# Two more up tiles computed in seven products, with a new order of the MLP and new places for the adding transfers

## The chip, the cores and the metric

The kernel runs on one core of a Trainium2 chip. The metric is the device time of one execution in microseconds. It was taken three times for the kernel before the change: 725.09, 725.68 and 725.84 us, with the median 725.68 us. One further execution was recorded by the hardware profiler; all rows below come from it.

## The reference

One layer of an encoder over 512 tokens of width 1024, all in float32: a norm, one input projection into three groups of attention heads, their attention, an output projection into the residual; then the MLP that the change touches, and a gated embedding of the input.

```python
def conv_gated_mlp(h, w_up, conv_w, conv_b, w_down):
    u = h @ w_up                                   # 512x1024 by 1024x5632
    up = jnp.pad(u, ((0, 0), (CONV_WIDTH - 1, 0), (0, 0)))
    c = conv_b
    for j in range(CONV_WIDTH):                    # causal, width 3, per channel
        c = c + conv_w[j] * up[:, j:j + S]
    gate, val = jnp.split(c, 2, axis=-1)
    return (jax.nn.silu(gate) * val) @ w_down      # 512x2816 by 2816x1024
...
    h = h + jnp.concatenate([o_a, o_b, o_c], axis=-1) @ w_out[i]
    h = h + conv_gated_mlp(rms_norm(h, ln_ffn[i]), w_up[i], conv_w[i], conv_b[i], w_down[i])
```

## The kernel before

**Products.** Each float32 operand is split into two parts of a narrower type: a rounded one (`hi`, made by ACT) and the remainder (`lo`, made by DVE). A product is three matmuls on PE: hi by hi, hi by lo, lo by hi. The weights come from DRAM into one of six raw tiles of 128x768 (`w_raw`), are split into `w_hi` and `w_lo`, and the raw tile is then free for the next load. Loads are issued by SP in one fixed order, each as soon as its raw tile is free.

**Up tiles.** The 2816 hidden channels are 22 tiles of 128. An up tile needs the 128 columns of the gate half and the 128 of the value half, for all 512 tokens. A plain tile (`up_plain`, accumulators named `u`) takes 2 halves x 8 blocks of rows x 3 = 48 matmuls that are 512 wide, and three raw tiles of weights (768, 768 and 512 columns). A tile in seven products (`up_seven`, accumulators `sX`, `sY`, `sZ`) sees the same work as a product of 2x2 block matrices (even and odd blocks of rows, gate and value, first and second half of the tokens) and takes seven block products in the place of eight: 7 x 4 x 3 = 84 matmuls that are 256 wide. It needs five raw tiles: two with the plain blocks, and three with sums of blocks (768, 768, 512 columns). The sums of the activations (`xh`, `xl`) are made once, whatever the number of such tiles. The results are put together by four copies on ACT and four additions on DVE into `su`, from which the convolution reads. Tiles 6 and 10 are computed so.

**Sums in DRAM.** The sums of weight blocks are not there at the start. Four transfers, DRAM to DRAM, issued by SP during the attention, copy blocks into a DRAM tensor (`usum` for an up tile, 4 x 256 KB; `dsum` for a phase of the down product, 4 x 768 KB or 4 x 512 KB). Later three transfers on POOL's queue add other blocks onto them in DRAM; the second and third read what the first has written. Before each, POOL runs a tiny `tok` instruction that reads the result of a finished up tile, so that the adding transfer does not start earlier. `COPY_SLOTS` (line 71) spreads all copies evenly over the units 20 to 45 of the attention; a copy stands in SP's order behind the last load issued by then (line 837). `ADD_AT` (line 72) gives for each add the number of finished up tiles behind which it stands.

**Down products.** Up tiles are taken together in four phases (tiles 0 to 5, 6 to 11, 12 to 17, 18 to 21), and each phase and half of the output columns is again seven products (`dn_X`, `dn_Y`, `dn_Z`), which are added to the residual `h` on DVE. Phase 0 makes its sums of weights on POOL (`w_raw<-w_raw,w_raw`), phases 1 to 3 read `dsum`.

**The order.** PE's order in the MLP is written out by hand in `ORDER` (line 49): a letter takes the next piece of a plain tile (P, three per tile), of a tile in seven products (S, six per tile) or of the down products (D, one product). Which tiles are plain follows from the same string (`tiles_of`, line 52). The orders of ACT, DVE, POOL and SP in the MLP follow from a planner at the end of the kernel: it gives each task a due time from PE's order and takes, again and again, the most urgent of those that could start. In the attention another scheduler sets the order. Nearly all instructions are recorded by a helper and carry its line, L108; the tiles' names tell them apart.

Of the kernel before, what the change touches and what calls it, by code (L numbers as in the profile page):

```python
# [45 lines left out]
PHASES = (0, 6, 12, 18, 22)  # L46


ORDER = ("PPPPPPPPPPPSSSPSSPSPPPDPDDDDDDPPPSSSSSDSDDDDDDPPPPPPPPPDPDDDDDDDPDPPDPPDDDDPPPPPPPPPPPPPPPPPPP")


def tiles_of(order):

    f, n, tiles = 2, {"P": 0, "S": 0}, {"P": [], "S": []}
    for c in order:
        if c in n:
            if n[c] == 0:
                tiles[c].append(f)
                f += 1
            n[c] = (n[c] + 1) % {"P": 3, "S": 6}[c]  # L60
    assert f == NF and not any(n.values()), (f, n)
    return tiles["P"], tiles["S"]


PLAIN, SEVEN = tiles_of(ORDER)

# [2 lines left out]
_sums = sorted([(f, "u", f) for f in SEVEN] + [(PHASES[ph + 1] + 3, "d", ph) for ph in range(NEAR, len(PHASES) - 1)])  # L69

COPY_SLOTS = (20, 46)
ADD_AT = (0, 0, 1, 1, 2, 2, 5, 5, 8, 9, 10, 12, 12, 12, 13)
COPIES, LATE = {}, {}
for _i, _q in enumerate(_sums):
    for _k in range(4):
        COPIES.setdefault(COPY_SLOTS[0] + (4 * _i + _k) * (COPY_SLOTS[1] - COPY_SLOTS[0]) // (4 * len(_sums)), []).append((_q[1:], _k))
    for _k in range(3):
        LATE.setdefault(ADD_AT[3 * _i + _k], []).append((_q[1:], _k))


@with_exitstack
def kernel(ctx: ExitStack, tc: tile.TileContext, x, xt0, xt, pt_in, small, g_ffn_in, bias_c,
# [1223 lines left out]
    def up_plain(f):  # L1306

        ws, w, more = plain_weights(f)
        us = Slot("z"), Slot("s")

        def some(g, ks):
            def do():
                c = g * NF + f
                if ks[0] == 0:
                    U[c] = bank("zs"[g], f"u{c}")
                for k in ks:
                    mm3(U[c], *w(g, k), Th[k // 4][:, k % 4, :], Tl[k // 4][:, k % 4, :], k == 0, k == KD - 1)
            return do

        for g in range(2):  # L1320
            pe_task(36, some(g, range(6)), [more()], (), [us[g]])
            yield
        last = []
        more()
        for g in range(2):
            last.append([pe_task(12, some(g, range(6, KD)), [ws[2]], (), (), [us[g]])])
        ff_chain(f, None, last, ((us[0],), (us[1],)))
        yield
# [213 lines left out]
    def down_pieces():  # L1542
        for ph in range(2):
            for n in range(2):
                d = Down((ph,), n, DT)
                for what in PRODUCTS:
                    d.product(what)
                    yield

        for n, whats in enumerate(FIRST):  # L1550
            DL.append(Down((2, 3), n, ({"X": "z", "Y": "s", "Z": "o"} if n else DT)))
            for what in whats:
                DL[n].product(what, (2,), False)
                yield

    DL = []
    pieces = {"P": (f for f in PLAIN for _ in up_plain(f)), "S": (f for f in SEVEN for _ in up_seven(f)), "D": down_pieces()}
    for c in ORDER:
        next(pieces[c])
# [231 lines left out]
```

## Time and profile before

| | before |
|---|---|
| median of three runs | 725.68 us |
| profiled execution | 725.56 us, of which the span is 723.8 us |
| PE busy | 706.4 us, 98% of the span |
| DVE, ACT, POOL busy | 536.2, 391.8, 220.2 us |
| mean granted clock | 0.996 |
| DMA queue of SP (q1) | 38,028 packets, 89.51 MB, 38.6% of 16 engines' span |
| DMA queue of POOL (q0) | 5,008 packets, 16.78 MB, 12.8% |
| attention until the first `u` matmul | 313.67 us |

The busy time of PE is modelled from pipelined matmuls, so its gaps are best read from the starts of neighbouring matmuls: 0.233 us apart when 512 wide, 0.119 us when 256 wide. A row of the chain or the timeline gives the start, the length, the engine and line, the operation and tiles; "[0.96 <-DMA ...]" is idle time ahead and what ended it. A row of a table of stretches gives the busy time of PE, PEld, DVE, ACT and POOL with the number of instructions, then the granted clock, the share of the DMA engines and GB/s.

### The profile page before, as it was taken

The numbers are of one execution on the slowest core, as the hardware profiler recorded it, in microseconds if no ns is written. First come the engines' busy times: TensorE is split into PE (matmuls) and PEld (weight loads), VectorE is DVE, ScalarE is ACT, GpSimd is POOL, SyncE is SP. The second block draws the span as 40 slices with busy tenths as digits, with TensorE's granted clock in tenths as the row PEclk, the third lists the DMA queues.
The fourth block names the chain that finished last, engine by engine and source line by source line (L and its number), as shares of the span: only waits on it lengthen the run. The fifth ranks groups of instructions, "written<-read, shape, count | busy, mean of one in ns | idle before, by whom it ended". The sixth has DMA issues, their size and how long they took to land.

```text
span 723.8 us, 11826 instructions
## 1 busy us (share of the span) xinstructions
PE 706.4 (98%) x4182; PEld 631.9 (87%) x4182; DVE 536.2 (74%) x1085; ACT 391.8 (54%) x739; POOL 220.2 (30%) x339
## 2 busy tenths in 40 slices
PE   9898999999999999999999999999999999999997
PEld 8897989988999887889889899988988888999886
DVE  8578787887878854857776998897857677677542
ACT  6646775865766663556354363645434445435721
POOL 4675675766665640200200505100010000000400
PEclk9999999999999999999999999999999999999999
DMA  9444446628414425563844463995595332742441
GB/s 328 176 138 115 123 118 164 204 66 265 131 57 140 146 49 169 161 227 61 190 106 137 96 226 83 242 200 182 167 236 158 94 91 88 234 143 82 156 130 56
DMA packets 43383, 107.35 MB, mean 148 GB/s; under 512 B 4886, under 2 KB 6550, under 8 KB 43324
## 3 DMA queue, kind: packets, MB, share of 16 engines
q1 hardware_dynamic: 38028, 89.51, 38.6%
q0 software_dynamic: 5008, 16.78, 12.8%
q8 instruction: 33, 0.54, 0.3%
q10 hardware_dynamic: 288, 0.30, 0.1%
q14 instruction: 26, 0.21, 0.1%
HBM read 98.31 MB, written 25.18 MB: 171 GB/s over the span
## 4 chain that ended last, share of the span: by engine, by line
PE 78%; DVE 10%; DMA 3%; ACT 3%; POOL 2%; issue 2%; SPq 0%; POOLq 0%; ACTq 0%; DVEq 0%
PE u L108 28%; PE dn_X L108 8%; PE C_z L108 6%; PE pg L108 6%; PE wo L108 5%; PE B_z L108 4%; PE dn_Y L108 4%; PE dn_Z L108 2%; PE A_z L108 2%; DVE w_lo L108 1%; DMA h<-in_x_dram 1%; PE pp L108 1%; PE C_s L108 1%; DVE A_e L108 1%; PE sX L108 1%
## 5 line engine op out<-in xcount | busy, mean ns | idle before, releaser
L108 PE MATMUL u<-Tl,w_hi 128*128 128x512 f32 (+1 forms) x352 | 131.9, 375 | 0.8 <-DVE Tl L108 0.8
L108 PE MATMUL u<-Th,w_hi 128*128 128x512 f32 (+1 forms) x352 | 131.9, 375 | 0.1
L108 PE MATMUL u<-Th,w_lo 128*128 128x512 f32 (+1 forms) x352 | 131.6, 374 | 0.0
L108 ACT CAST w_hi<-w_raw 128x768 fp32r<-128x768 f32 (+1 forms) x116 | 88.6, 786 | 73.2 <-PE u L108 32.4
L108 DVE TENSOR_TENSOR w_lo<-w_raw,w_hi 128x768 fp32r<-128x768 f32 (+1 forms) x116 | 106.5, 933 | 27.5 <-ACT w_hi L108 27.4
L108 DVE SCALAR_TENSOR_TENSOR c<-u,cols,c 128x511 f32<-128x511 f32 x80 | 59.6, 747 | 26.4 <-ACT c L108 25.2
L108 PEld LDWEIGHTS u<-Tl,w_hi 128*128 128x128 f32 x352 | 66.0, 188 | 13.9 <-DVE Tl L108 1.2
L108 PEld LDWEIGHTS u<-Th,w_lo 128*128 128x128 f32 x352 | 66.0, 188 | 13.2
L108 PEld LDWEIGHTS u<-Th,w_hi 128*128 128x128 f32 x352 | 66.0, 188 | 13.1 <-ACT pps L108 0.5
L233 POOL TENSOR_SCALAR rstd<-rstd 128x1 f32<-128x1 f32 x12 | 2.6, 216 | 155.2 <-ACT n_sq L108 154.8
L108 ACT ACTIVATE c<-u,cols 128x512 f32<-128x512 f32 x40 | 31.0, 776 | 29.1 <-PE u L108 29.1
L108 PE MATMUL dn_X<-w_hi,g_ah 128*128 128x256 f32 x144 | 40.6, 282 | 0.4 <-ACT c L108 0.4
L108 PE MATMUL dn_X<-w_hi,g_al 128*128 128x256 f32 x144 | 40.4, 281 | 0.0
L108 PE MATMUL dn_X<-w_lo,g_ah 128*128 128x256 f32 x144 | 40.4, 280 | 0.0
L108 POOL TENSOR_TENSOR w_raw<-w_raw,w_raw 128x768 f32<-128x768 f32 x8 | 15.5, 1938 | 67.1 <-DVE w_lo L108 56.4
L108 PE MATMUL B_z<-B_h,Th 128*128 128x384 f32 x96 | 34.6, 360 | 0.6 <-DVE B_zn L108 0.6
L108 POOL TENSOR_SCALAR tok<-c 128x1 f32<-128x1 f32 x15 | 7.7, 510 | 90.1 <-DVE c L108 90.1
L108 PE MATMUL C_z<-C_h,Th 128*128 128x384 f32 x96 | 34.3, 357 | 0.0
L108 PE MATMUL C_z<-C_h,Tl 128*128 128x384 f32 x96 | 32.3, 337 | 0.0
L108 PE MATMUL B_z<-B_h,Tl 128*128 128x384 f32 x96 | 32.3, 337 | 0.0
L108 PE MATMUL C_z<-C_l,Th 128*128 128x384 f32 x96 | 32.3, 336 | 0.0
L108 PE MATMUL B_z<-B_l,Th 128*128 128x384 f32 x96 | 32.3, 336 | 0.0
(488 smaller groups left out, 2107.0 us busy)
## 6 DMA issues: line engine op xcount, KB each, us to landing
w_raw<-in_w_up_dram SPq DMA_DIRECT2D x44, 384.0 KB, 4.7
w_raw<-in_w_down_dram SPq DMA_DIRECT2D x20, 384.0 KB, 3.6
dsum<-in_w_dsum_dram SPq DMA_DIRECT2D x8, 768.0 KB, 7.0
w_raw<-dsum SPq DMA_DIRECT2D x16, 384.0 KB, 3.7
w_raw<-in_w_up_dram SPq DMA_DIRECT2D x20, 256.0 KB, 4.7
B_r<-in_w_in_dram SPq DMA_DIRECT2D x12, 384.0 KB, 3.4
C_r<-in_w_in_dram SPq DMA_DIRECT2D x12, 384.0 KB, 4.1
wo_r<-in_w_out_dram SPq DMA_DIRECT2D x16, 256.0 KB, 3.0
```

The lines of the kernel that those rows point to most:

```text
L108: ins = getattr(self.eng, op)(*a, **k)
L233: nc.gpsimd.tensor_scalar(r[:, 1:2], r[:, 0:1], 1.0 / D, EPS, ALU.mult, ALU.add)
```

## The change

Two tables of numbers are replaced. By the new `ORDER` four up tiles, 6, 10, 15 and 17, are in seven products, and the pieces of tiles and down products stand in other places. There are two more sums of weights (`usum` of tiles 15 and 17), so 28 copies and not 20 are spread over the same units, and six adds more stand in `ADD_AT`.

```diff
-ORDER = ("PPPPPPPPPPPSSSPSSPSPPPDPDDDDDDPPPSSSSSDSDDDDDDPPPPPPPPPDPDDDDDDDPDPPDPPDDDDPPPPPPPPPPPPPPPPPPP")
+ORDER = ("PPPPPPPPPPPSSPSSPSPSPPPDDDDDPDDPPSSSDSPSDSDDDDPDPPPPPPPDDDDDDDDDDDPPDDDPPSSSSSPSPPSSSPSSPSPPPPPPPPPP")
...
 COPY_SLOTS = (20, 46)
-ADD_AT = (0, 0, 1, 1, 2, 2, 5, 5, 8, 9, 10, 12, 12, 12, 13)
+ADD_AT = (0, 0, 0, 1, 2, 5, 5, 6, 7, 8, 9, 9, 9, 11, 11, 11, 12, 15, 16, 16, 16)
```

On SP, at the end of the attention, before (`wo` are the weights of the output projection; the first digit is the block of rows, the second the half of the columns):

```order
L838 DMA dsum3_3369<-in_w_dsum3_dram 128x1024
L108 DMA wo5_1_r_3668<-in_w_out_dram 128x512
L838 DMA dsum3_3369<-in_w_dsum3_dram 128x1024
L108 DMA wo6_0_r_3731<-in_w_out_dram 128x512
L108 DMA wo6_1_r_3762<-in_w_out_dram 128x512
L108 DMA wo7_0_r_3795<-in_w_out_dram 128x512
```

and with the change:

```order
L838 DMA dsum3_3563<-in_w_dsum3_dram 128x1024
L108 DMA wo5_1_r_3677<-in_w_out_dram 128x512
L838 DMA dsum3_3563<-in_w_dsum3_dram 128x1024
L108 DMA wo6_0_r_3740<-in_w_out_dram 128x512
L838 DMA dsum3_3563<-in_w_dsum3_dram 128x1024
L108 DMA wo6_1_r_3772<-in_w_out_dram 128x512
```

The last of the 512-KB copies of `dsum3` now stands behind the load of `wo6_0_r`; before, its four copies stood behind the loads wo5_0, wo3_1, wo4_1 and wo5_1.

On DVE, in phase 0 of the down products, ahead of the addition of the third X product to `h`, before (`c28` and `c7` are taps of the convolution, `dn0_0` is phase 0, first half of the columns):

```order
L108 TENSOR_TENSOR h_63<-h_63,dn0_0_X_4919 128x2x256
L108 SCALAR_TENSOR_TENSOR c28_5081<-su6_1_4763,cols_83,c28_5081 128x511
L108 SCALAR_TENSOR_TENSOR c7_5085<-u7_4798,cols_83,c7_5085 128x511
L108 TENSOR_TENSOR w_lo5_4098<-w_raw2_3862,w_hi5_4097 128x768
L108 SCALAR_TENSOR_TENSOR c7_5085<-u7_4798,cols_83,c7_5085 128x510
L108 TENSOR_TENSOR h_63<-h_63,dn0_0_X_4919 128x2x256
```

and with the change:

```order
L108 TENSOR_TENSOR h_63<-h_63,dn0_0_X_4953 128x2x256
L108 SCALAR_TENSOR_TENSOR c6_5044<-su6_0_4760,cols_83,c6_5044 128x510
L108 TENSOR_TENSOR w_lo5_4110<-w_raw2_3874,w_hi5_4109 128x768
L108 SCALAR_TENSOR_TENSOR c28_5108<-su6_1_4775,cols_83,c28_5108 128x511
L108 SCALAR_TENSOR_TENSOR c7_5112<-u7_4792,cols_83,c7_5112 128x511
L108 TENSOR_TENSOR h_63<-h_63,dn0_0_X_4953 128x2x256
```

The split `w_lo5` now stands two taps (`c28`, `c7`) ahead of that addition, before one (`c7`). On PE, the last 12 matmuls of tile 8 (6 of each half, 512 wide) now stand between the third X product and the last two products of this group (Y and the fourth X); before they stood behind the group.

On POOL, the adds from tile 9 on, with the change (the rows of `dsum2` stand for phase 2; `c9` and `c11` are the results of tiles 9 and 11):

```order
L108 TENSOR_SCALAR tok_4100<-c9_5363 128x1
L108 DMA usum15_2627<-usum15_2627 128x512
L108 TENSOR_SCALAR tok_4100<-c9_5363 128x1
L108 DMA usum17_2867<-in_w_up17_dram 128x1024
L108 TENSOR_SCALAR tok_4100<-c11_5656 128x1
L108 DMA dsum2_3224<-in_w_dadd2_dram 128x2x1536
L108 TENSOR_SCALAR tok_4100<-c9_5363 128x1
L108 DMA usum15_2627<-usum15_2627 128x512
L108 TENSOR_SCALAR tok_4100<-c11_5656 128x1
L108 DMA usum17_2867<-usum17_2867 128x512
```

Before, POOL had nothing between the adds of `dsum1` and `dsum2` here; now the adds of `usum15` and `usum17` stand among them, and those of `dsum3` and the last of `dsum2` stand behind tiles 15 and 16 and not 12 and 13.

## The prediction

> **What bounds the kernel now.** I read the page first for the busy shares, then the chain of waits, PE's list of waits, and the timelines of the two places that the change touches.
>
> ```profile
> PE 706.4 (98%) x4182; PEld 631.9 (87%) x4182; DVE 536.2 (74%) x1085; ACT 391.8 (54%) x739; POOL 220.2 (30%) x339
> PE 78%; DVE 10%; DMA 3%; ACT 3%; POOL 2%; issue 2%; SPq 0%; POOLq 0%; ACTq 0%; DVEq 0%
> PE wo L108 <- DMA wo_l<-wo_r: 1.0, 1, 1.0
> ```
>
> PE is busy for 98% of the span and makes up 78% of the chain. Its one wait for a DMA in the output projection is 1.0 us. So the time falls when PE has less to do or loses one of these waits, and rises when PE gets a new wait; the other engines count only where PE is made to wait for them. This is the chain from the one stall in the MLP on:
>
> ```profile
> 419.84 4.81 DMA w_raw<-in_w_up_dram
> 424.73 0.84 ACT w_hi L108
> 426.93 2.37 PE dn_X L108 x18
> 429.30 11.20 PE u L108 x48
> 440.50 1.42 PE sX L108 x12
> ...
> 499.07 2.11 PE dn_X L108 x18
> ```
>
> From 426.93 on it is PE alone, piece after piece. Up to there a load that came late ends it.
>
> **PE's work.** The change turns tiles 15 and 17 from plain ones into tiles of seven products. A plain one is the row of 48 matmuls, 11.20 us (0.233 us each). The pieces of tile 10 stand in the same window of the chain:
>
> ```profile
> 441.92 2.85 PE sZ L108 x24
> 444.76 1.44 PE sY L108 x12
> 446.20 1.44 PE sX L108 x12
> 447.64 1.43 PE sY L108 x12
> 449.07 2.16 PE dn_X L108 x18
> 451.23 1.44 PE sX L108 x12
> ```
>
> With the sX of 440.50 and without the dn_X this is 1.42 + 2.85 + 1.44 + 1.44 + 1.43 + 1.44 = 10.02 us for 84 matmuls, 0.119 us each. A tile gains 11.20 − 10.02 = 1.18 us, two gain 2.36. All else on PE is as before in number: 28 down products, the attention in its old order. I take −2.36, bounds −2.5 to −2.3 from the rounding of seven rows.
>
> Will matmuls half as wide still hide their loads of weights?
>
> ```profile
> L108 PEld LDWEIGHTS sX<-xh,w_hi x16: 187/188/193, 389.5 to 452.0; 128*128 128x128 f32 x16
> 440.00:460.00 20.00, 20.00 (x169) 19.91 (x168) 16.29 (x23) 8.10 (x14) 5.36 (x5) 1.00 0.61 129
> ```
>
> A weight load is recorded with 188 ns and yet the matmuls follow at 119 ns; in this stretch, mostly of 256-wide work, PEld is full (19.91 of 20) and PE too. So the loads overlap one another, and the price of 10.02 us already holds them. The Trainium skill ("TensorE: Matmul & The Clock Gate", section "Back-to-back issue gap") says that in a sustained stream the weight load and the matmul set the spacing together, about 81 ns at 128 columns and 131 ns at 512. On the line between these two, my estimate for 256 columns is 98 ns; by it a tile of seven would take 84 × 98 = 8.2 us and a plain one 48 × 131 = 6.3, so the change would lose 1.9 us a tile. The trace has 10.02 against 11.20 and disagrees in both spacings.
>
> **The stall at 426 us.** Ahead of the third X product PE starts nothing for 426.93 − 426.26 = 0.67 us, 0.55 more than the pitch of 0.12:
>
> ```profile
> 426.26 0.28 PE L108 MATMUL dn_Y<-w_hi,g_al 128*128 128x256 f32 x1
> 426.93 0.35 PE L108 MATMUL dn_X<-w_hi,g_ah 128*128 128x256 f32 x1 [0.39 <-ACT c L108]
> 424.57 0.96 DVE L108 TENSOR_TENSOR w_lo<-w_raw,w_hi 128x768 fp32r<-128x768 f32 x1 [1.36 <-ACT w_hi L108]
> ...
> 426.11 0.68 DVE L108 TENSOR_TENSOR h<-h,dn_X 128x512 f32<-128x512 f32 x1
> ```
>
> The profile names ACT, but the last step before PE is DVE's addition to `h` (426.11 + 0.68 = 426.79), which frees the accumulator of the product before. It is late because DVE waited 1.36 us for ACT's `w_hi`, and that for the load issued at 419.84. The change puts half of tile 8 (12 matmuls of 0.233 us, 2.8 us) between the third X and the two products behind it, spreads the group's products over more time, and puts two taps and not one between the split and the addition. With 2.8 us of other work for an accumulator to come free I expect the stall to go: −0.55. The other end is 0: the load is late at another place, and the next product pays.
>
> **The copy beside the output projection.** There are eight copies more, 28 over the same units of the attention. I weigh only the last 512 KB of `dsum3`, which now stands right behind the load of `wo6_0_r`:
>
> ```profile
> 268.39 6.14 SPq L108 DMA_DIRECT2D wo_r<-in_w_out_dram  x4
> 268.05 6.66 DMA wo_l<-wo_r
> 273.40 0.40 PE L108 MATMUL wo<-wo_h,Th 128*128 128x512 f32 x1
> 274.76 0.50 PE L108 MATMUL wo<-wo_l,Th 128*128 128x512 f32 x1 [0.96 <-DMA wo_l<-wo_r]
> DMA to landing us min/median/max: 3.4/4.6/6.7
> ```
>
> SP issues those loads from 268.39, just when POOL has issued the last of four transfers that make `wo_l`. That one takes 6.66 us, lands at 274.71, and PE starts its reader at 274.76, 1.36 − 0.23 = 1.13 us later than it could. The landings of the four grow from 3.4 to 6.7 us, so the DMA engines are full, as the stretches show:
>
> ```profile
> 245.00:250.00 5.00, 5.00 (x32) 4.23 (x32) 3.96 (x8) 3.05 (x7) 1.84 (x4) 1.00 0.94 329
> 265.00:270.00 5.00, 5.00 (x28) 4.22 (x27) 1.10 (x3) 3.85 (x8) 3.45 (x4) 1.00 0.77 124
> 270.00:275.00 5.00, 4.04 (x22) 3.02 (x21) 1.66 (x3) 1.26 (x3) 0.00 (x0) 1.00 0.97 243
> 280.00:300.00 20.00, 20.00 (x90) 16.19 (x89) 14.63 (x22) 9.33 (x17) 4.20 (x7) 1.00 0.44 145
> ```
>
> At the rate of the first row (329 GB/s at a share of 0.94, so 350 GB/s when full) 512 KB keep all engines for 1.5 us. If all of that goes ahead of the last `wo_l`, PE waits 1.5 us more; if the queue of SP has it wait behind the loads, nothing. No gain is possible, since nothing is taken away there. PE is full afterwards (20.00 of 20 in the last row), so a delay is carried to the end. I take +0.8, about half, because two queues feed the same engines. The Trainium skill ("DMA: Bandwidth & Descriptors", section "Queues, rings and completion order") says that a DMA engine goes round between its queues packet by packet; by that the copy takes its share while the adding transfer runs, which is what the growth of the landings from 3.4 to 6.7 us looks like, and the end of 1.5 is the nearer one.
>
> The other seven copies lie in stretches where PE waits for no transfer (the list of waits above has only the `wo_l` one), so I set them at 0. Without that cover, each 256 KB would cost 0.75 us.
>
> **What the new tiles ask of the others.** Two raw tiles of weights more for each (five, not three), four copies and four additions:
>
> ```profile
> L108 DVE TENSOR_TENSOR w_lo<-w_raw,w_hi 128x768 fp32r<-128x768 f32 x90 | 89.0, 999 | 23.5 <-ACT w_hi L108 23.4
> L108 ACT CAST w_hi<-w_raw 128x768 fp32r<-128x768 f32 x90 | 73.6, 834 | 63.0 <-PE u L108 27.6 <-PE dn_X L108 12.3 <-PE dn_Y L108 7.4
> L108 DVE TENSOR_TENSOR su<-sX,su x8: 408/420/425, 384.7 to 459.5; 128x256 f32<-128x256 f32 x8
> L108 ACT COPY su<-sZ x4: 372/372/373, 384.3 to 444.8; 128x256 f32<-128x256 f32 x4
> ```
>
> DVE gets 2 × 1.0 + 4 × 0.42 = 3.7 us a tile, ACT 2 × 0.834 + 4 × 0.372 = 3.2. They fall into the stretches of late up tiles:
>
> ```profile
> 540.00:560.00 20.00, 20.00 (x123) 17.75 (x122) 14.16 (x23) 8.96 (x13) 0.81 (x1) 1.00 0.64 175
> ...
> 580.00:600.00 20.00, 20.00 (x88) 16.05 (x87) 14.16 (x23) 10.38 (x15) 0.00 (x0) 1.00 0.30 90
> ```
>
> DVE has 5.84 us free in the first and the last, 11.7 together, against 7.4; ACT 20 against 6.4. So 0 on PE's path; with no free time the cover would be gone and DVE would set 3.7 us a tile. The transfers:
>
> ```profile
> q1 hardware_dynamic: 38028, 89.51, 38.6%
> q0 software_dynamic: 5008, 16.78, 12.8%
> ```
>
> SP's queue costs 0.386 × 723.8 / 89.51 = 3.1 us of all engines for a MB, POOL's 0.128 × 723.8 / 16.78 = 5.5. Four raw tiles more (1.57 MB) are 4.9 us, six adding transfers more (2.1 MB) 11.6 us. The two stretches above alone have 7.2 and 14.0 us of the engines free, so there is room for the 16.5. I take 0; the loss is the third rival's.
>
> **The sum.** −2.36 − 0.55 + 0.8 = −2.1 us against the profiled execution of 725.56, so 723.5; that one lies 0.12 under the median of 725.68, so **723.6** as a median.
>
> **The rivals.** (1) The copy takes its full price and the stall only moves: −2.36 + 1.5 = −0.9, 724.8. For it: the engines at 0.97 in 270 to 275. Against it: two mishaps at once, and the 2.8 us of tile 8.
>
> (2) The copy costs nothing, because SP's loads issued around it keep the engines full as before and it lies behind the last `wo_l`: −2.9, 722.8. Against it: it is issued less than a microsecond after that transfer, which then has over 6 us to go.
>
> (3) The other side: weights come late in the new block of eleven down products without an up piece among them (at most eight before). Each product takes 2.13 us (the row of 499.07 has 2.11) and one raw tile of 384 KB; with six raw tiles a tile comes round every 12.8 us, of which its casts and splits take 0.83 + 1.0. So it decides when a landing takes over 11.0 us. The nearest row, for the raw tiles from 440 to 560:
>
> ```profile
> DMA to landing us min/median/max: 3.0/4.9/10.4
> 460.00:480.00 20.00, 20.00 (x110) 17.14 (x109) 18.46 (x30) 12.23 (x19) 1.62 (x3) 1.00 0.91 235
> ```
>
> The longest, 10.4, is near, and this stretch with down products already runs at 0.91. Two adding transfers of the new tiles (512 and 256 KB, 0.786 MB × 5.5 = 4.3 us) beside it make 14.7, 3.7 us too late: −2.1 + 3.7 = +1.6, 727.3. Against it: the median is 4.9, PE lost nothing in that stretch (20.00 of 20), and the split weights made ahead take up a first delay.
>
> (4) The narrow matmuls cost more than the wide ones save, at the 8.2 and 6.3 us above: two tiles +3.8 in the place of −2.36, 729.8. The rows of 10.02 and 11.20 speak against it.
>
> **How the numbers follow.** The forecast has 0.55, with its own range from 722.9 to 724.5; rival 1 0.20, rival 2 0.12, rival 3 0.12, rival 4 0.01. A measurement of this kernel can tell about 0.2% from no change, 1.45 us, so faster is below 724.2 and slower above 727.1. Faster takes nine tenths of the forecast, rival 2 and a little of rival 1: 0.64. Same takes the rest of those two and the small form of rival 3: 0.23; slower the most of rival 3, rival 4 and what I do not see: 0.13. The range of 722.2 to 726.2 holds the forecast, rivals 1 and 2 up to their edges, and the smaller half of rival 3.
>
> **What would show it.** Two rows of 48 plain matmuls less and pieces of sX, sY, sZ at 1.43 us behind 500 us: the first term. No start-gap over 0.3 us ahead of the third X of phase 0: the second. PE's wait on `wo_l` at 1.8 us where it was 1.0, with a landing near 7.5: the third; 1.0 would be rival 2, 2.5 rival 1. A first `u` matmul 0.8 us later than 313.67 would say the same. PE waiting for `w_lo` or `w_hi` between dn_X, dn_Y and dn_Z in 460 to 520 would be rival 3, and so would a wait of sX on a sum that lands late behind 560. The prediction is wrong, whatever the total, if PE gets a wait over 1 us at a place that I have not named.

## The result, and the profile after

The changed kernel takes 730.19 us (median of five runs, 729.63 to 733.08) against 725.68 us: a ratio of 1.0069 with a 95% interval of 1.0046 to 1.0091. It is slower by 0.7%, where −0.3% was forecast. Taken once more, with the kernel before beside it, it was 730.56 us against 724.94, 1.0080 (1.0064 to 1.0096). One execution among those of the experiments below, of the kernel with both losses away and the new copies in gaps, took 981.35 us at a mean granted clock of 0.656: it counts in that kernel's median of five (722.28 us, and 721.76 without it), not in its ratio. The profiled execution took 729.63 us, its span 727.9 against 723.8.

The page after, busy times and DMA queues:

```profile
PE 705.8 (97%) x4254; PEld 635.3 (87%) x4254; DVE 540.1 (74%) x1097; ACT 398.3 (55%) x751; POOL 228.8 (31%) x353
q1 hardware_dynamic: 39756, 93.18, 39.7%
q0 software_dynamic: 5872, 18.88, 14.7%
```

PE is busy for about as long as before, though two tiles cost less: something made matmuls longer. The list of what PE waited for has two entries at its head that are new or longer:

```profile
PE dn_X L108 <- DVE h L108: 3.1, 1, 3.1
PE wo L108 <- DMA wo_l<-wo_r: 2.8, 1, 2.8
```

The first did not exist before; the second was 1.0 us. The wait at 426.93 us, ahead of the fourth X of phase 0 (0.4 us before), is no longer in the list. The weight loads of the plain up tiles, first and last start, before and then after:

```profile
L108 PEld LDWEIGHTS u<-Th,w_hi x352: 186/188/193, 313.7 to 620.0; 128*128 128x128 f32 x176
```

```profile
L108 PEld LDWEIGHTS u<-Th,w_hi x320: 186/188/193, 316.5 to 624.7; 128*128 128x128 f32 x160
```

The MLP's up part starts 2.8 us later and takes 308.2 us where it took 306.3: 1.9 more, and not the 2.9 less of the first two terms. The chain of waits after, at its two new places and at the first new tile of seven products:

```profile
268.49 8.48 DMA wo_l<-wo_r
...
501.53 12.91 DMA w_raw<-dsum
514.55 0.84 ACT w_hi L108
...
517.12 6.03 PE dn_X L108 x36
...
549.88 1.42 PE sX L108 x12
551.30 2.85 PE sZ L108 x24
554.14 1.44 PE sY L108 x12
555.58 1.44 PE sX L108 x12
557.02 1.42 PE sY L108 x12
...
562.65 1.44 PE sX L108 x12
```

The tile of seven products costs 10.01 us, as forecast. But a load took 12.91 us to land, and the 36 matmuls behind it took 6.03 us where 36 × 0.119 is 4.28. The stretches of PE, PEld, DVE, ACT and POOL around it, with the granted clock and the DMA share:

```profile
500.00:520.00 20.00, 16.86 (x129) 16.45 (x128) 12.49 (x16) 7.21 (x10) 0.00 (x0) 0.94 0.98 244
...
514.00:516.00 2.00, 0.00 (x0) 0.00 (x0) 0.59 (x1) 1.32 (x2) 0.00 (x0) 1.00 1.05 313
516.00:518.00 2.00, 0.89 (x6) 0.92 (x7) 2.00 (x4) 1.87 (x4) 0.00 (x0) 0.91 0.91 324
518.00:520.00 2.00, 2.00 (x11) 2.00 (x11) 1.90 (x3) 1.22 (x2) 0.00 (x0) 0.50 0.78 257
520.00:522.00 2.00, 2.00 (x15) 2.00 (x14) 1.09 (x2) 0.84 (x1) 0.00 (x0) 0.74 0.92 298
```

PE stands still, and then runs at a granted clock of 0.50 for over 3 us. So the wait is paid twice: 3.3 us of standing (the start-gap, from the start of one matmul to that of the next, of 3.42 less the pitch) and 1.75 us of slow matmuls. What kept the DMA engines at 0.98 shows in POOL's timeline:

```profile
493.38 0.23 POOL L108 TENSOR_SCALAR tok<-c 128x1 f32<-128x1 f32 x1 [23.21 <-DVE c L108]
493.83 1.19 POOL L108 DMA_DIRECT2D dsum<-in_w_dadd_dram  x1 [0.22 <-issue]
494.59 0.68 POOL L108 TENSOR_SCALAR tok<-c 128x1 f32<-128x1 f32 x1
494.83 1.27 POOL L108 DMA_DIRECT2D usum<-usum  x1
495.43 0.90 POOL L108 TENSOR_SCALAR tok<-c 128x1 f32<-128x1 f32 x1
495.62 1.49 POOL L108 DMA_DIRECT2D usum<-usum  x1
```

The first add of `dsum2` (1.57 MB) waited 23 us for the result of tile 11, and the adds of `usum15` and `usum17` (256 KB each) queued behind it on POOL. All three then started within 1.8 us, 5 to 7 us ahead of the eleven down products (the first starts at 501.0). And this is what DVE did there:

```profile
511.95 0.96 DVE L108 TENSOR_TENSOR w_lo<-w_raw,w_hi 128x768 fp32r<-128x768 f32 x1 [1.92 <-ACT w_hi L108]
515.41 0.96 DVE L108 TENSOR_TENSOR w_lo<-w_raw,w_hi 128x768 fp32r<-128x768 f32 x1 [2.51 <-ACT w_hi L108]
516.29 0.68 DVE L108 TENSOR_TENSOR h<-h,dn_X 128x512 f32<-128x512 f32 x1
```

The profile's releaser of the wait is the last row, the addition to `h` that frees an accumulator for the seventh of the eleven products. It stood behind two splits of late weights.

The span's difference of 4.1 us, put together: the first up matmul 2.8 us later (1.8 of it the longer wait on `wo_l`; the other 1.0 may be scatter, since in the experiments below whose wait on `wo_l` is 0.9 to 1.0 us, plain up work starts anywhere from 313.1 to 315.0 us), the up part 1.9 us longer, and the rest 0.6 shorter. The 1.9 is −2.36 − 0.55 by the forecast, + 3.3 + 1.75 for the wait and the slow matmuls, which makes 2.1.

### The profile page after: what moved, and what is told of

Read it like the earlier page. It is cut to its first block, busy times and chain, and to the rows that moved or that the text cites. A ratio compares the mean times of both kernels' runs of the same rounds, so it can differ in the third digit from the quotient of the medians.

```text
span 727.9 us, 12027 instructions
## 1 busy us (share of the span) xinstructions
PE 705.8 (97%) x4254; PEld 635.3 (87%) x4254; DVE 540.1 (74%) x1097; ACT 398.3 (55%) x751; POOL 228.8 (31%) x353
## 4 chain that ended last, share of the span: by engine, by line
PE 78%; DVE 9%; DMA 5%; ACT 3%; POOL 2%; issue 2%; SPq 0%; POOLq 0%; DVEq 0%; ACTq 0%
PE u L108 23%; PE dn_X L108 7%; PE C_z L108 6%; PE pg L108 6%; PE wo L108 5%; PE B_z L108 4%; PE A_z L108 4%; PE dn_Y L108 3%; PE sX L108 2%; DMA w_raw<-dsum 2%; PE sY L108 2%; PE sZ L108 2%; PE dn_Z L108 2%; PE pp L108 1%; PE A0b_z L108 1%
## 5 line engine op out<-in xcount | busy, mean ns | idle before, releaser
L108 ACT CAST w_hi<-w_raw 128x768 fp32r<-128x768 f32 (+1 forms) x120 | 91.2, 787 | 75.2 <-DMA w_raw<-in_w_up_dram 17.0
L108 PE MATMUL u<-Th,w_hi 128*128 128x512 f32 (+1 forms) x320 | 119.4, 373 | 0.7 <-ACT pps L108 0.7
L108 PE MATMUL u<-Tl,w_hi 128*128 128x512 f32 (+1 forms) x320 | 119.2, 372 | 0.8 <-DVE Tl L108 0.8
L108 PE MATMUL u<-Th,w_lo 128*128 128x512 f32 (+1 forms) x320 | 118.9, 372 | 0.0
L108 PEld LDWEIGHTS u<-Tl,w_hi 128*128 128x128 f32 x320 | 60.0, 188 | 12.1 <-DVE Tl L108 1.2
L108 PEld LDWEIGHTS u<-Th,w_hi 128*128 128x128 f32 x320 | 60.0, 188 | 12.0 <-ACT pps L108 1.1
L108 PEld LDWEIGHTS u<-Th,w_lo 128*128 128x128 f32 x320 | 60.0, 188 | 11.8
L108 DVE SCALAR_TENSOR_TENSOR c<-u,cols,c 128x511 f32<-128x511 f32 (+1 forms) x72 | 53.4, 746 | 17.5 <-ACT c L108 16.5
L108 POOL TENSOR_SCALAR tok<-c 128x1 f32<-128x1 f32 x21 | 10.5, 498 | 147.9 <-DVE c L108 147.9
L108 ACT ACTIVATE c<-u,cols 128x512 f32<-128x512 f32 x36 | 27.8, 776 | 16.3 <-PE u L108 16.3
```

The lines of the kernel that those rows point to most:

```text
L108: ins = getattr(self.eng, op)(*a, **k)
```

## The experiments

Medians, with the kernel before run beside them on the same chip. The first row is the result above (before: 725.68 us). The four rows behind it ran together (before: 725.16), as did the next four (before: 725.65) and the last three (before: 724.94).

| kernel | us | ratio to before (95%) | PE's wait on `wo_l`, us | longest landing of a raw tile's load from 490 to 525 us, us |
|---|---|---|---|---|
| changed | 730.19 | 1.0069 (1.0046 to 1.0091) | 2.8 | 13.0 |
| adds of `dsum2` later | 725.53 | 0.9999 (0.9990 to 1.0008) | 2.6 | 4.1 |
| last copy earlier | 728.31 | 1.0046 (1.0033 to 1.0060) | 0.9 | 13.6 |
| both, new copies in gaps | 722.28 | 0.9959 (0.9945 to 0.9972) | 0.9 | 4.6 |
| new order, two tiles only | 724.23 | 0.9988 (0.9980 to 0.9997) | 0.9 | 8.2 |
| block broken up | 732.78 | 1.0099 (1.0085 to 1.0112) | 2.5 | 13.5 |
| before, adds bunched | 725.55 | 1.0000 (0.9990 to 1.0010) | 1.0 | 13.1 |
| before, last copy late | 729.49 | 1.0050 (1.0035 to 1.0065) | 3.1 | 6.3 |
| both, copies as changed | 722.42 | 0.9951 (0.9938 to 0.9963) | 1.0 | 4.6 |
| additions to `h` first | 725.62 | 1.0010 (0.9998 to 1.0022) | 2.8 | 13.3 |
| additions first, last copy earlier | 722.03 | 0.9961 (0.9947 to 0.9974) | 1.0 | 12.8 |
| changed, once more | 730.56 | 1.0080 (1.0064 to 1.0096) | 2.7 | 13.9 |

**The adds moved out of the block.**

```diff
-ADD_AT = (0, 0, 0, 1, 2, 5, 5, 6, 7, 8, 9, 9, 9, 11, 11, 11, 12, 15, 16, 16, 16)
+ADD_AT = (0, 0, 0, 1, 2, 5, 5, 6, 7, 8, 9, 9, 9, 11, 11, 13, 13, 15, 16, 16, 16)
```

> The changed kernel with the first two adds of dsum2 behind tile 13 and not 11 and 12, so that 1.57 MB of the adding transfers no longer run beside the loads of the eleven down products. Theory A (the three adds issued together from 493.8 to 495.6 made the loads late: 12.9 us for the load issued at 501.5): the wait of 3.3 us ahead of the down product falls below 0.5 us, the slow matmuls behind it (36 at up to 0.213 us, 1.8 us in all) go with it, and the median is 730.2 - 5.1 = 725.1. Rival B (six raw tiles are too few for eleven down products in a row, adds or not): a wait over 2 us stays in the block, the median is 728 or more.

725.53 us: 4.7 us less than the changed kernel. The two small adds no longer stand behind that of `dsum2` and start at 476.2 and 493.7 us. The loads in the block landed within 4.1 us and PE had no wait left in the MLP above 0.5 us. DVE's order up to 526 us is that of the changed kernel: the additions stand behind the same splits, and with prompt loads this costs nothing. So the bunch of adds is a necessary part of the loss, and eleven down products in a row are not too many for six raw tiles. The longer wait on `wo_l` stayed, and here the granted clock fell behind that one:

```profile
274.00:276.00 2.00, 0.31 (x1) 0.30 (x2) 0.93 (x3) 0.05 (x1) 0.00 (x0) 1.00 1.01 382
276.00:278.00 2.00, 2.00 (x8) 1.59 (x7) 0.83 (x2) 0.62 (x1) 0.00 (x0) 0.78 0.51 169
278.00:280.00 2.00, 2.00 (x6) 1.52 (x6) 0.46 (x1) 0.00 (x0) 0.00 (x0) 0.50 0.43 142
```

**The last copy moved back.**

```diff
+COPIES[44].append(COPIES.pop(45)[0])
```

> The changed kernel with the last 512-KB copy of dsum3 back behind the load of wo5_1 (beside the third one), all else the same. Theory A (this copy shares the DMA engines with the last wo_l transfer): PE's wait on wo_l falls from 2.8 back to about 1.0 us and the median by 1.8 us, to 728.4; if the 0.56 us that PE lost later, ahead of the first up matmul, came from the same delay, to 727.8. Rival C (the eight copies more as a whole keep the engines behind, wherever the last one stands): the wait stays above 2 us and the median above 729.5.

728.31 us, 1.9 less. The waits of PE:

```profile
PE dn_X L108 <- DVE h L108: 4.2, 1, 4.2
...
PE wo L108 <- DMA wo_l<-wo_r: 0.9, 1, 0.9
```

The copy's place is the whole of the second loss; eight copies more, elsewhere, leave this wait at 0.9. The wait in the block, which this edit doesn't touch, varies: 4.2 us here, 3.1 and 5.0 in the two profiles of the changed kernel.

**Both, with the new copies in the gaps of the old ones.** Beside the edit of `ADD_AT`, `COPIES` is written out:

```diff
+COPIES = {}
+for _key, _slots in ((("u", 6), (20, 21, 22, 23)), (("u", 10), (25, 26, 27, 29)), (("d", 1), (30, 31, 33, 34)),
+                     (("d", 2), (35, 36, 38, 39)), (("d", 3), (40, 42, 43, 44)),
+                     (("u", 15), (24, 28, 32, 37)), (("u", 17), (36, 38, 39, 41))):
+    [COPIES.setdefault(_s, []).append((_key, _k)) for _k, _s in enumerate(_slots)]
```

> The changed kernel with the adds of dsum2 behind tile 13, and the twenty copies of before in their old units, the eight new ones in units 24, 28, 32, 36, 37, 38, 39 and 41; POOL's order at the select of the fourth bias block is then that of before. Theory A (three mishaps: the adds beside the block, the last copy beside wo_l, the select ahead of two moves of B1_k0; the rest of the change pays as forecast): 725.7 - 2.36 - 0.55 = 722.8, with no PE wait in the MLP over 0.5 us. Rival B: 725 or more, with a wait over 2 us in the block. Rival D (PE's saving of 1.18 us a tile does not come): 725 without such a wait.

722.28 us, faster than the kernel before by 0.4%. With both losses gone, the four tiles pay about what the first two terms say: 2.9 us below the 725.16 of the same chip, 2.9 forecast.

**The new order with two tiles only.** Tiles 15 and 17 plain (their twelve S in `ORDER` become six P), the adds of the other five sums where the change puts them, the copies of before.

> The changed order of the MLP and the changed places of the adds, but tiles 15 and 17 plain: no usum of theirs, so only two seven-product tiles and the twenty copies of before. Theory A: only the first add of dsum2 (1.57 MB) runs beside the block of eleven, the two of usum do not; in the trace of before that add landed 12.7 us after its issue and the loads beside it 10.4, under the 11.0 that decides, so PE waits 0 to 1 us there; with the stall of 0.55 gone: 725.1 to 726.2. Rival B: a wait over 2 us stays in the block, 728 or more. The difference to the kernel with four seven-product tiles and neither mishap is 2.4 us by the forecast's first term.

724.23 us, a little better than expected. The 1.57 MB of `dsum2` started behind tile 11 as in the changed kernel, but alone; loads took up to 8.2 us, and PE did not wait. Against the kernel with four such tiles, on the same chip, this is 1.95 us slower by the medians and 2.1 by the ratios: the measure of the first term, where 2.36 was forecast and the intervals leave about 1 us either way. (The two kernels also differ in the first adds of `dsum2`, behind tile 11 here and 13 there; PE waits for neither.)

**The block broken up.**

```diff
-... "PPPPPPPDDDDDDDDDDDPPDDDPPSSSSS" ...
+... "PPPPPPPDPDDDDDDDPDPDDDDDPSSSSS" ...
```

> The changed kernel with its adds where they are, but with the block of eleven down products broken up as before: one product, a third of an up tile, seven products, a third, one product, a third, five products, a third. Theory A (it is the rate at which PE asks for raw tiles against the rate at which loads land beside 2.1 MB of adds): the up third that comes in after the first product gives the loads 2.8 us more, so the wait of 3.3 us falls to 0.5 to 1.5 and the slow matmuls behind it go: 725.8 to 727.5. Rival E (the late landing alone sets it, the order of the block is of no account): a wait of 3 us or more and 729.5 or more.

Theory A was wrong here, and so in part was the reason given for the first experiment: the wait grew to 4.5 us and the time to 732.78. A third of an up tile inserted behind the first product should have given the loads time. DVE's timeline shows why it did not:

```profile
515.98 0.96 DVE L108 TENSOR_TENSOR w_lo<-w_raw,w_hi 128x768 fp32r<-128x768 f32 x1 [2.00 <-ACT w_hi L108]
516.85 0.68 DVE L108 TENSOR_TENSOR h<-h,dn_X 128x512 f32<-128x512 f32 x1
```

Again the addition that PE waited for stands behind a split whose load took 13 us. In this profile what stands ahead of the addition on DVE mattered more than 2.8 us of other work on PE.

**The kernel before with its adds bunched.**

```diff
-ADD_AT = (0, 0, 1, 1, 2, 2, 5, 5, 8, 9, 10, 12, 12, 12, 13)
+ADD_AT = (0, 0, 1, 1, 2, 2, 5, 5, 8, 11, 12, 12, 11, 12, 13)
```

> The kernel before, its order of the MLP untouched (at most eight down products in a row), but the first adds of dsum2 and of dsum3 (1.57 and 1.05 MB) both behind tile 11. Theory A: 2.6 MB beside the loads of phase 1 is more than the 2.1 MB of the changed kernel, loads land 13 us or later after their issue, and PE waits 2 us or more among the products of phase 1; the median rises by 2 to 6 us, to 727.5 to 731.5. Rival B (only eleven in a row ask too much): no wait over 0.5 us, 725 to 726.

Also against theory A: loads landed as late as 13.1 us after their issue, and yet the time did not change (725.55). PE's waits:

```profile
PE dn_X L108 <- ACT w_hi L108: 0.9, 1, 0.9
```

Here the wait is for the weights themselves (`w_hi`), and it is under 1 us. So late landings alone cost little here. It is not quite the same case: the adds start 12 us ahead of the first product of phase 1 (486.4 and 498.4 us), 7 in the changed kernel, and where an addition does stand behind a late split (at 502.77, after DVE waited 4.0 us), PE has 2.8 us of an up tile to do before it needs the accumulator. This led to a new theory, H: the weights come nearly in time; PE waits because the planner, which counts on a load 2 us after its transfer, put splits of late weights ahead of the addition in DVE's order.

**The kernel before with the last copy late.**

```diff
+COPIES[45] = [COPIES[44].pop()]
```

> The kernel before with one thing moved: the last 512-KB copy of dsum3 stands behind the load of wo6_0, as in the changed kernel. Theory A: PE's wait on wo_l rises from 1.0 to 2.6 to 2.8 us and the median by 1.6 to 1.8, to about 727.2; where the wait makes PE slow for some microseconds behind it, as in one profile with a start-gap of 3.0 us, up to 1.4 more. Rival C (eight copies more are needed for it): the wait stays at 1.0 and the time at 725.5.

729.49 us, 3.8 more than before, where 1.6 to 1.8 was expected and 3.2 with the slow clock: all from one transfer of 512 KB moved by one unit. The wait on `wo_l` was 3.1 us, and the clock stayed down for 6.8 us; in this profile the first `u` matmul starts at 318.5 us and not 313.7:

```profile
274.00:276.00 2.00, 0.00 (x0) 0.00 (x0) 1.45 (x3) 0.56 (x2) 0.00 (x0) 1.00 0.99 372
276.00:278.00 2.00, 1.32 (x3) 1.13 (x4) 0.00 (x0) 0.53 (x1) 0.00 (x0) 0.51 0.53 191
278.00:280.00 2.00, 2.00 (x6) 1.52 (x6) 0.46 (x1) 0.00 (x0) 0.00 (x0) 0.50 0.43 142
280.00:282.00 2.00, 2.00 (x7) 1.52 (x6) 0.00 (x0) 0.00 (x0) 0.00 (x0) 0.50 0.31 113
282.00:284.00 2.00, 2.00 (x8) 1.61 (x7) 0.00 (x0) 0.00 (x0) 0.00 (x0) 0.78 0.00 0
```

**Both losses taken away, the copies as in the change.** The edits of the first two experiments together.

> The changed kernel with the adds of dsum2 behind tile 13 and the last copy beside the third; the copies otherwise as in the changed kernel, so POOL's select of the fourth bias block stays ahead of the two moves of B1_k0. Theory A: the two mishaps are all there is, the select costs nothing in most runs: the same as the kernel with the eight copies in the gaps, 722.3, within 0.4. Rival F (the select costs 0.6 us each time, as in the profile of the changed kernel): 722.9 or more, and a start-gap over 0.6 us above the pitch ahead of B_s near 150 us.

722.42 us, the same as with the copies in the gaps. The place of POOL's select, which comes ahead of two moves here as in the changed kernel, costs nothing that these runs can tell. In the profiles with this order PE's waits for those moves (`B_k_k`) near 148 us range from none, as here, to 1.1 us in the kernel with the additions first and the last copy earlier; in the changed kernel it is 0.2.

**The additions to `h` first.** The planner's trial is told that loads in a window of 16 us take longer; the adds and copies stay as in the change.

```diff
-        return at_, t0 + (2.0 if q.kind not in ("pe", "do") and q.parts[-1][1] else 0.0), c
+        return at_, t0 + ((9.0 if q.kind == "load" and 182 < t0 < 198 else 2.0) if q.kind not in ("pe", "do") and q.parts[-1][1] else 0.0), c
```

DVE's order in phase 1 in the changed kernel (the addition of 516.29 is the fourth row):

```order
L108 TENSOR_TENSOR w_lo6_4115<-w_raw5_4107,w_hi6_4114 128x768
L108 TENSOR_TENSOR w_lo0_3865<-w_raw0_3862,w_hi0_3864 128x768
L108 TENSOR_TENSOR w_lo1_3871<-w_raw1_3868,w_hi1_3870 128x768
L108 TENSOR_TENSOR h_63<-h_63,dn1_0_X_5733 128x2x256
L108 TENSOR_TENSOR w_lo2_3877<-w_raw2_3874,w_hi2_3876 128x768
L108 TENSOR_TENSOR h_63<-h_63,dn1_0_Y_5754 128x2x256
```

and in this one:

```order
L108 TENSOR_TENSOR w_lo6_4115<-w_raw5_4107,w_hi6_4114 128x768
L108 TENSOR_TENSOR h_63<-h_63,dn1_0_X_5733 128x2x256
L108 TENSOR_TENSOR w_lo0_3865<-w_raw0_3862,w_hi0_3864 128x768
L108 TENSOR_TENSOR h_63<-h_63,dn1_0_Y_5754 128x2x256
L108 TENSOR_TENSOR w_lo1_3871<-w_raw1_3868,w_hi1_3870 128x768
L108 TENSOR_TENSOR w_lo2_3877<-w_raw2_3874,w_hi2_3876 128x768
```

> The changed kernel, its adds and its copies where they are; only the planner is told that loads started in 16 us of the block land 9 us and not 2 us after they have been moved. It then puts DVE's additions to h of the products X and Y of phase 1 ahead of the two splits (w_lo0, w_lo1) that wait for the late loads; the orders of SP and PE, and the order of the adds, stay. Theory H (the weights come in time; PE waits since the addition that frees the accumulator stands behind two splits of late weights in DVE's order): from the timestamps of the changed kernel the addition could run at 511.7 and not 516.3, and the next two products' weights were split at 512.9 and 516.4, ahead of their use at 515.9 and 518.1. So the wait of 3.3 us falls below 0.7 and the slow matmuls behind it go: 730.2 - 5 = 725.2. Rival A (the weights themselves come too late for PE, whatever DVE does first): a wait of 2 us or more stays in the block, 729 or more.

725.62 us, 4.9 less than the changed kernel on the same chip (730.56). The three adds still start together and loads still land up to 13.3 us after their issue. DVE's timeline at the two additions:

```profile
512.84 0.96 DVE L108 TENSOR_TENSOR w_lo<-w_raw,w_hi 128x768 fp32r<-128x768 f32 x1 [0.64 <-ACT w_hi L108]
513.72 0.68 DVE L108 TENSOR_TENSOR h<-h,dn_X 128x512 f32<-128x512 f32 x1
515.62 0.96 DVE L108 TENSOR_TENSOR w_lo<-w_raw,w_hi 128x768 fp32r<-128x768 f32 x1 [1.22 <-ACT w_hi L108]
516.49 0.68 DVE L108 TENSOR_TENSOR h<-h,dn_Y 128x512 f32<-128x512 f32 x1
```

The orders of PE, SP and POOL in this trace are those of the changed kernel; about a dozen rows of DVE's and four of ACT's stand elsewhere. Theory H holds in the main: the same late loads cost 4.9 us with one order of DVE's queue and little with another. With the first experiment, which keeps DVE's order in the block and has prompt loads, this shows that the loss takes both: late loads, and additions behind their splits. Not all went as expected: in this profile, of an execution of 728.31 us, a wait of 1.3 us was left behind 522 us, in which an addition again stood behind a split; below 0.7 was expected.

**The same with the last copy earlier.**

> The same, and the last copy of dsum3 beside the third, so that both costs are taken away with the adds left in the block. Theory H: 722.4, as with the adds moved behind tile 13, within 0.7, and no wait over 0.7 us in the MLP. Rival A: 726 or more.

722.03 us, 0.4% faster than before, with the adds left in the block. PE's wait on `wo_l` is 1.0 us, as before the change. The stretch of the block:

```profile
500.00:520.00 20.00, 19.97 (x169) 19.80 (x168) 15.19 (x21) 7.48 (x10) 0.00 (x0) 1.00 0.98 260
```

The DMA engines are as full as in the changed kernel (0.98), loads land up to 12.8 us after their issue, and PE stays busy (19.97 of 20).

**The changed kernel once more.**

> The changed kernel once more, on the chip of the two others, as their measure: 729.5 to 731, PE's waits of about 3 us on wo_l and in phase 1 both there, and matmuls at half speed for 3 us or longer behind one of them or both.

730.56 us, as expected. In the profile taken here the wait on `wo_l` is 2.7 us and the one in the block larger, 5.0:

```profile
PE dn_X L108 <- DVE h L108: 5.0, 1, 5.0
```

Three versions beat both kernels, by 0.4 to 0.5%, and cannot be told apart: 722.03, 722.28 and 722.42 us.

## Why the prediction was wrong

*PE's work, −2.36*: right. The tile takes 10.01 us in the profile after, and four tiles against two are worth about 2 us in time (1.95 by the medians, 2.1 by the ratios).

*The stall at 426 us, −0.55*: right in size, but not shown to be for the reason given. The stall is gone from PE's list. It stood ahead of the fourth X of phase 0, not the third (the X products before start at 409.41, 417.84, 422.07 and 426.93 us). In the profile after, DVE does not wait ahead of the split in question (at 424.40 us), and the addition of the third X is done at 427.98. Without the twelve matmuls of tile 8 the fourth X would have come at about 429.2 (an estimate: the third X ends at 427.09, and Y is 18 matmuls at 0.119 us). So the load that came in time was enough, and the 2.8 us of other work were not needed, as far as this profile shows: that the term came out is in part luck.

*The copy beside the output projection, +0.8 (0 to 1.5)*: the place and the mechanism were right, the size was not. The wait rose by 1.8 us, above the upper end, and in the kernel before with the last copy late 3.8 us of time followed. SP's timeline after shows the copy 0.7 us behind the issue of the last `wo_l`:

```profile
269.18 1.23 SPq L838 DMA_DIRECT2D dsum<-in_w_dsum_dram  x1
```

That `wo_l` then landed 8.48 us after its issue and not 6.66, 1.8 more: the bound of 1.5, from the bytes of the copy at a rate of another stretch, was too low by 0.3. What the sum lacked wholly is the slow clock that can follow a wait.

*"I take 0; the loss is the third rival's"*: this is the step that failed, the term that put the new adds at nothing. The room for the transfers was reckoned as free DMA time over 20-us stretches behind 540 us, but five of the six new adds were issued before 496 us, two of them together with the first add of `dsum2`. In the place of the 0 the profile after shows 5.05 us, 3.3 of standing and 1.75 of slow matmuls. The rows of POOL's order ahead of the prediction already showed the add of `dsum2` for tile 11 standing ahead of `usum15`'s for tile 9: an in-order queue turns three adds with different due places into one bunch. In time this is 4.7 us by the experiment that takes the bunch out of the block and 4.9 by the one that puts the additions first (by the ratios to the kernel before 5.1 in both). Of the 6.6 us between the forecast and the median, 5.05 are this loss and 1.0 is the wait on `wo_l`, which grew by 1.8 and not 0.8; the last 0.5 is not traced.

*Rival 3* (chance 0.12, 727.3) had the right place, and its first half came true: a landing of 12.9 us where 11.0 was to decide. But its reason, that six raw tiles run out, is not what PE waited for. With the loads just as late, but the additions first, PE had one wait of 1.3 us in one profile and none in the other. The price (3.7 us) was near the standing time of 3.3 us, again without the slow matmuls.

The prediction had described this very mechanism for the stall at 426 us: an addition to `h` that is late since DVE waits ahead of it for a split of a late load. It was looked for at the one place where it cost time before, and not at the places where the change makes loads late.

## What to carry to other kernels

A transfer that is hidden by the free time of a stretch must be checked where it is issued: find what it waits for, what is queued behind it, and whether they start together. Late data hurts first where an in-order engine has put work on it ahead of work that another engine is waiting for, so a plan that counts on prompt loads should place the steps that free accumulators first. And a wait of PE of 3 us or so is priced with what comes after it: here the clock was at half speed behind most of them, for 3.4 or 6.8 us.

## What was not expected of the hardware

*The clock after a wait.* In these profiles PE's granted clock fell to 0.50 behind start-gaps of 2.9 to 5.3 us: behind 3.4 us here (matmuls of 256 columns 0.213 us apart and not 0.119), behind 3.0 us in the kernel with the adds later, behind 3.5 us in the one with the last copy late. It did not behind the gap of 3.18 us on `wo_l` in the profile of the changed kernel, and at gaps of up to 1.6 us nowhere in the MLP. The traces show what tells them apart. The stretches at 0.50 last 3.41 or 6.83 us, and within a trace all changes of the clock lie whole multiples of 3.413 us apart: in the changed kernel the fall at 517.63 us comes 142.0 of them behind one at 32.94. On this grid, the changed kernel at its two gaps, and then the kernel with the adds later:

```profile
275.28:278.70 3.42, 1.68 (x7) 1.41 (x8) 1.06 (x3) 0.62 (x1) 0.00 (x0) 1.00 0.78 271
278.70:282.11 3.41, 3.41 (x16) 2.80 (x16) 1.06 (x2) 0.00 (x0) 0.00 (x0) 1.00 0.35 122
514.22:517.63 3.41, 0.52 (x4) 0.55 (x5) 2.22 (x3) 2.82 (x4) 0.00 (x0) 1.00 0.98 314
517.63:521.04 3.41, 3.41 (x18) 3.41 (x17) 2.40 (x5) 1.72 (x4) 0.00 (x0) 0.50 0.85 283
```

```profile
273.69:277.11 3.42, 1.42 (x6) 1.20 (x7) 1.24 (x3) 0.95 (x2) 0.00 (x0) 1.00 0.82 300
277.11:280.52 3.41, 3.41 (x10) 2.64 (x9) 1.29 (x2) 0.03 (x1) 0.00 (x0) 0.50 0.41 144
```

The gap of 3.18 us is cut by the grid, so that PE stands 1.7 us in the stretch shown and less in the one ahead, and the clock stays. The gap of 3.0 us leaves 2.0 us of standing in one stretch, and the next one is at 0.50. In the 13 traces (their last 10 us left out) a stretch with 2.0 us of standing or more was always followed by half clock, one with 1.5 or less never; of three with 1.6 to 1.75 two were. Half clock went on for a second stretch where PE stood 0.63 us or more in the first (three cases), and ended where it stood 0.56 or less. So whether a wait of about 3 us costs only itself depends on where it falls. The Trainium skill ("TensorE: Matmul & The Clock Gate", section "What's actually happening") says that the array's clock is halved after an idle window of about 3.4 us, and that the window runs freely and does not start anew with the kernel. The halving and the free-running window agree; that 2.0 us of standing in a window were enough is less than the idle window stated. That the place of the wait on the grid decides also fits the spread of executions of one kernel: of the six with the last copy late, the two fastest (727.80 and 728.37 us) have a mean granted clock of 0.998, the three slowest (730.12 to 730.80) 0.994.

*Adds in DRAM beside loads.* The loads issued beside the three adds, from 498.9 to 505.8 us, landed 9 to 13 us after their issue; in the kernel with the adds later none of 490 to 525 us took more than 4.1. From 500 to 520 us POOL's queue moved 1.36 MB in 40.1% of the engines' time and SP's 3.48 MB in 57.5%, together the 0.98 that the stretch shows. This makes 5.9 us and 3.3 us of all engines for a MB, so the prediction's prices of 5.5 and 3.1 were nearly right; what it had wrong was when they are paid. The load issued at 498.86 us landed at 508.11, behind the add of 1.57 MB, which was issued 5 us ahead of it and landed at 506.5. That a load waits for most of the bytes issued ahead of it on the other queue fits this, but no run tests it.
